# The reciprocal square roots of ten norms moved from GpSimd to ScalarE and VectorE, and two products to other PSUM banks, in a four-layer encoder trunk on one core

## The chip, the cores and the metric

The kernel runs on one core of one Trainium2 chip. The metric is the device time of one execution in microseconds (us). Three runs of the kernel before took 1830.92, 1827.35 and 1828.51 us, a median of 1828.51 us. The engines are named as the profile names them: PE (TensorE products), PEld (TensorE weight loads), DVE (VectorE), ACT (ScalarE), POOL (GpSimd), SP (SyncE, which issues the transfers).

## The reference

512 tokens of width 1024 pass through two layers. Each layer is half a SwiGLU, a mixer, and another half SwiGLU, and every one of these begins with an RMS norm over the width:

```python
def rms_norm(x, g):
    return x * rsqrt(mean(x * x, axis=-1) + 1e-6) * g
def swiglu(x, w_gate, w_up, w_down):          # 1024 -> 2816 -> 1024
    return (silu(x @ w_gate) * (x @ w_up)) @ w_down
for layer in range(2):
    h = h + 0.5 * swiglu(rms_norm(h), ...)
    h = h + mixer[layer](rms_norm(h), ...)    # 0: pooling and forgetting attention
    h = h + 0.5 * swiglu(rms_norm(h), ...)    # 1: latent attention, with two norms inside
out = rms_norm(h)
```

The mixer of layer 0 joins pooled means with 8 heads of attention whose logits carry sums of log forget gates (one Sigmoid per frame and head). That of layer 1 is attention with 16 heads over a compressed query (256 wide) and compressed keys and values (128 wide); each of the two has an RMS norm of its own. All is float32.

## The kernel before

Activations lie with the width on the 128 partitions (8 chunks, `h`) and the 512 tokens along the columns. Float32 products are made from two parts of each operand, a rounded one and the rest: `hi` is an ACT copy (L158), `lo` a DVE subtraction (L163, L165), and `mm3` issues three PE products for a block (L176 to L178). Weights come by SP in runs of 8 blocks (`raw`, three buffers), and are split by `split` or, in the feed-forward phases, by `unit`. In a part of the mixers' weights the subtraction is made on POOL instead (L205).

A norm's factor is not applied to the input of a projection but to its sums in PSUM, so that products can start before it is known. ACT squares each chunk of `h` as it becomes final, POOL (for the last chunk DVE) adds the squares up in `acc`, and `sums` turns them into the factor: products with a column of ones bring the sums to the tokens' partitions (L363), DVE divides and adds epsilon (L374), POOL raises to the power -0.5 (L375); `spread` then copies the factor to all partitions by products with the identity (L381) and an ACT copy to `rstdB` (L385). There are ten such norms: one ahead of each of the four feed-forward phases and two mixers, two inside the latent attention, and two at the end, where the output is normed in halves of the tokens. In the two at the end the last chunk's squares are not added to `acc` but summed by products of their own, and DVE adds the two sums (L370).

A feed-forward phase (`ffn`) makes gate and up products of two chunks of 128 hidden units at a time. The first pair of chunks is made by plain products: `begin` in the first phase, whose four sums lie in banks `pa`, `pa`, `px`, `pz`; `eight` in the other three, where all four sums take the two banks `pa` in turn, so that an up sum can start only when a gate sum has been read by DVE, times `rstdB` (L519). The other ten pairs are made by seven products of half size (`seven`, banks `px`, `py`, `pz`). Their right-hand factors (`right_factors`: L564 on ACT, L568 to L571 on DVE, and their splits) are made from `h` while the first pair's products run. Down products go to `pa` and are added to `h` by DVE (L602).

The order on each engine is made by the framework's list scheduler, which plays the program through a time model of its own, takes what is ready by priority (`soon` moves a step 400 places ahead), and then fixes the order of each engine's queue; at run time a queue waits at its head. `issue_after` adds an order behind a given instruction on that instruction's engine: the weights of the later pairs of heads in the latent attention (`keys_values`) have their POOL subtractions behind the last power. There `ordered` also fixes the order of products to the program's.

ACT holds one table of functions at a time. The profile shows seven ACT_TABLE_LOAD: one at the start (L222), three for Silu (L649), one each for Sigmoid (L870) and Exp in the two mixers (L784, L1250).

Of the kernel before, what the change touches and what calls it, by code (L numbers as in the profile page):

```python
# [34 lines left out]
# columns of the array of small parameters  # L35
# [22 lines left out]
# the order of the 1024 rows' chunks in a run of gate or up weights: pairs (2p, 2p + 1) of chunks  # L58
# are halves of the contraction
K_ORDER = (0, 2, 4, 6, 1, 3, 5, 7)  # L60
H = S // 2
# how much sooner than in the program's order the sums in PSUM are read
SOON = 400
# pairs of heads whose outputs are projected together, and how many chunks after a head's scores
MLA_GROUPS = ((0, 2), (2, 4), (4, 8))
EARLY = 1
# pairs of hidden chunks whose products are summed over together
GROUPS = ((0,), (1, 2), (3, 4), (5, 6), (7, 8), (9, 10))

# the causal layout of a head's 1280 score columns over three banks:  # L70
# query block -> (bank, first column)
SCORE_AT = ((1, 384), (2, 0), (1, 0), (0, 0))
# key block -> (bank, first column) of the transposed probabilities
PT_AT = ((0, 0), (1, 0), (2, 0), (1, 384))
PT_COLS = (512, 512, 256)
# forgetting attention: what the streamed column chunks are, and after which
# head's scores each of them is projected
# [9 lines left out]
def side_by_side(tile):  # L87
    """The two parts of the values of pairs of heads: [hi | lo] of one, [lo | hi] of the other."""
    v = tile.rearrange("p s n -> p (s n)")[:, 0:S].rearrange("p (q s c) -> p q s c", s=4, c=64)
    return v[:, :, ::3, :], v[:, :, 1:3, :]  # L90


# the banks of PSUM: rings of them in the feed-forward phases, and what the mixers take of them
# [4 lines left out]
class Trunk:  # L98
    def __init__(self, ctx, tc, d, out):
# [3 lines left out]
        self.pending = self.ordered = False  # L103
        self.state = ctx.enter_context(tc.tile_pool(name="state", bufs=1))
# [16 lines left out]
    @contextmanager  # L121
    def behind(self):
        """Work to be issued after that on the last chunk of the norm's input."""
        with ExitStack() as stack:
            for ins in self.last:
                stack.enter_context(self.tc.issue_after(ins.ins))
            yield
# [15 lines left out]
    def banks(self, **tags):  # L143
        """What a phase's kinds of sums take in turn of the banks."""
# [24 lines left out]
    def pe(self, ins):  # L169
        """Where the products' order is the program's."""  # L170
# [40 lines left out]
    def unit(self, src, blocks=8, piece=8, pool=False):  # L211
        """A run of 128x128 weight blocks from DRAM, split in two float32r parts."""
        return self.split(self.load(src, piece, blocks), piece, blocks, pool)

# [1 line left out]
    def setup(self):  # L216
        nc, d = self.nc, self.d
        k = self.keep
        # the table of activation functions comes in ahead of the data
        self.warm = k([P, 1], F32, "warm")  # L220
        nc.gpsimd.memset(self.warm, 0.0)
        nc.scalar.activation(self.warm, self.warm, AF.Copy)  # L222
# [3 lines left out]
        self.nhalf = k([P, TB], F32, "nhalf")  # L226
        nc.gpsimd.memset(self.nhalf, -0.5)
# [7 lines left out]
    def setup_tables(self):  # L235
        nc, d, k = self.nc, self.d, self.keep
        # tri[p, s] = 1 where p <= s
# [7 lines left out]
        # causal[p, s] = MASKED where s > p  # L245
# [9 lines left out]
        # sel8[p, h] = 1 where p is h, 32 + h, 64 + h or 96 + h  # L255
# [8 lines left out]
        # 1 over the counts of the pooling windows' first frames  # L264
# [9 lines left out]
    def rope_tables(self):  # L274
        """rope = [cos; +-sin; +-sin; cos], 32 rows each, frames along the columns: the steps."""
# [5 lines left out]
            # chunked[p, s] = MASKED where p < 64 <= s  # L281
# [31 lines left out]
        def angles():  # L313
            # cos(r) = sin(pi/2 - |r|)
# [15 lines left out]
    def square_into(self, src, first, last=False, part=slice(0, S)):  # L330
        """The last chunk's squares are kept apart: the sum over partitions takes both."""
# [14 lines left out]
    def prep(self, c, col):  # L346
        """Chunk c of h, times the norm's weight, in two parts."""
# [4 lines left out]
    def stats(self, n, rstdB):  # L352
        """From the squares: rsqrt(mean + eps), per token on partitions and as rows."""
        return self.sums(n)(rstdB)

    def sums(self, n):
        """The first part of it; what it returns does the second."""
# [3 lines left out]
        for i, sq in enumerate(self.squares):  # L361
            for t in range(blocks):
                self.pe(nc.tensor.matmul(ps[:, t * n_sq + i : t * n_sq + i + 1],  # L363
                                         sq[:, t * P : (t + 1) * P], self.ones[:, 0:1],
                                         start=True, stop=True))
        rt = self.ring("rt", 3, (P, TB))[:, 0:blocks]
        sums = ps[:, 0 : blocks * n_sq]
        if n_sq > 1:
            both = self.ring("both", 1, (P, TB))[:, 0:blocks]
            nc.vector.tensor_reduce(  # L370
                both, sums.rearrange("p (t i) -> p t i", i=n_sq), op=ALU.add, axis=AX.X
            )
            sums = both
        nc.vector.tensor_scalar(rt, sums, 1.0 / n, EPS, op0=ALU.mult, op1=ALU.add)  # L374
        self.power = nc.gpsimd.tensor_tensor(rt, rt, self.nhalf[:, 0:blocks], op=ALU.pow)  # L375

        def spread(rstdB):
            # every partition's copy of the tokens' values, by the identity
# [12 lines left out]
    def settle(self):  # L391
        """The norm that the last stage left to this one."""
        if self.pending:
            self.pending = False
            with self.soon():
                return self.stats(D, self.rstdB)

# [1 line left out]
    def ffn(self, f, col, next_col, start=False, rope=False):  # L399
        """Gate and up products of two chunks of 128 hidden units at a time, by Winograd's form of  # L400
        Strassen's seven products (but for the first two); the down products of a group of
# [1014 lines left out]
```

## Time and profile before

| what | us |
|---|---|
| median of three runs | 1828.51 (1827.35 to 1830.92) |
| the profiled execution: first to last instruction (its span) | 1824.4 |
| what lies between that span and the median | 4.1 |
| PE busy | 1753.3 |
| DVE busy | 1492.0 |
| ACT busy | 912.7 |
| POOL busy | 235.2 |

The profile comes from one execution; of that execution only the span is given, so the 4.1 us hold what lies around the span and the difference of one execution from the median. In a row of the timeline the first number is the start from the beginning of the span, the second the length; what stands in brackets is the idle time of that engine just before, and what ended it. `x3` is the number of instructions merged. The clock is that granted to TensorE, 1.00 being 2.4 GHz and 0.50 the lower level of 1.2 GHz; a window with 0.75 had each for half of its length.

### The profile page before, as it was taken

Reading aid. Unit: us, or ns where it says so; the run is one execution under the profiler, and the core shown is the slowest. Engines: PE = TensorE matmul, PEld = TensorE weight load, DVE = VectorE, ACT = ScalarE, POOL = GpSimd, SP = SyncE. Lnnn points to the kernel's source line nnn. Section 1 sums busy time; section 2 is a strip of 40 time slices with the busy share of each in tenths; the row PEclk is TensorE's granted clock in tenths of the full one; section 3 lists DMA queues with packets and bytes.
Section 4 is the critical chain, followed back from the end, with each engine's and each line's share of the span. In section 5 each row is a group of like instructions: output and inputs, shape, how many; then the busy total and the mean of one; then the engine's idle time right before and its main releaser. Section 6 shows DMA issues by size and latency. Waiting matters only on the chain.

```text
span 1824.4 us, 28424 instructions
## 1 busy us (share of the span) xinstructions
PE 1753.3 (96%) x11324; PEld 1585.1 (87%) x11324; DVE 1492.0 (82%) x2367; ACT 912.7 (50%) x1486; POOL 235.2 (13%) x165
## 2 busy tenths in 40 slices
PE   5999999999998999999999999999799989999998
PEld 4999999888787999999889999998677779999997
DVE  7998888648968988887779998964999789888873
ACT  6554444446645544444545444534677554444443
POOL 4000000113351000000200000003544310000002
PEclk8999999999999999999999999999999999999999
DMA  4233333313122333333223333241211123333331
GB/s 152 93 119 113 96 109 109 98 43 96 59 81 58 116 116 96 106 100 121 84 75 110 105 104 105 93 129 34 59 29 53 58 59 116 116 102 106 96 103 47
DMA packets 48933, 167.06 MB, mean 92 GB/s; under 512 B 5536, under 2 KB 7584, under 8 KB 48800
## 3 DMA queue, kind: packets, MB, share of 16 engines
q1 hardware_dynamic: 48800, 165.25, 30.0%
q8 instruction: 88, 1.44, 0.3%
q14 instruction: 45, 0.37, 0.1%
HBM read 163.14 MB, written 2.10 MB: 91 GB/s over the span
## 4 chain that ended last, share of the span: by engine, by line
PE 82%; DVE 10%; issue 3%; POOL 2%; ACT 2%; DMA 0%; SPq 0%; DVEq 0%; POOLq 0%; ACTq 0%
PE pa L176 11%; PE pa L177 11%; PE pa L178 11%; PE px L178 8%; PE px L176 8%; PE px L177 8%; PE pz L178 4%; PE pz L176 4%; PE pz L177 4%; PE py L178 2%; DVE pr L791 2%; PE py L176 2%; PE py L177 2%; POOL rt L375 2%; DVE mn L781 1%
## 5 line engine op out<-in xcount | busy, mean ns | idle before, releaser
L158 ACT ACTIVATE wh<-raw 128x1024 fp32r<-128x1024 f32 (+2 forms) x228 | 231.2, 1017 | 186.8 <-PE pa L177 77.0
L163 DVE TENSOR_TENSOR wl<-raw,wh 128x1024 fp32r<-128x1024 f32 (+1 forms) x195 | 234.5, 1205 | 24.7 <-ACT wh L158 24.1
L344 POOL TENSOR_TENSOR acc<-acc,sq 128x512 f32<-128x512 f32 (+1 forms) x48 | 63.0, 1313 | 1040.2 <-ACT sq L338 1039.7
L602 DVE SCALAR_TENSOR_TENSOR h<-pa,h 128x512 f32<-128x512 f32 (+1 forms) x200 | 132.8, 666 | 63.9 <-PE pa L178 62.7
L176 PE MATMUL pa<-hh,wh 128*128 128x512 f32 (+1 forms) x400 | 153.2, 383 | 0.0
L177 PE MATMUL pa<-hl,wh 128*128 128x512 f32 (+1 forms) x400 | 153.1, 383 | 0.0
L178 PE MATMUL pa<-hh,wl 128*128 128x512 f32 (+1 forms) x400 | 153.0, 383 | 0.0
L158 ACT ACTIVATE vh<-raw 128x1024 fp32r<-128x1024 f32 x88 | 93.2, 1059 | 88.9 <-PE px L177 37.4
L178 PE MATMUL px<-xh,wl 128*128 128x256 f32 (+1 forms) x456 | 129.9, 285 | 0.1
L177 PE MATMUL px<-xl,wh 128*128 128x256 f32 (+1 forms) x456 | 129.0, 284 | 0.0
L176 PE MATMUL px<-xh,wh 128*128 128x256 f32 (+1 forms) x456 | 128.8, 284 | 0.0
L177 PE MATMUL pa<-hl,vh 128*128 128x512 f32 (+1 forms) x336 | 128.0, 381 | 0.0
L176 PE MATMUL pa<-hh,vh 128*128 128x512 f32 (+1 forms) x336 | 127.7, 382 | 0.0
L158 ACT ACTIVATE wh<-s 128x1024 fp32r<-128x1024 f32 (+1 forms) x52 | 52.2, 1008 | 149.8 <-PE px L177 114.1
L178 PE MATMUL pa<-hh,vl 128*128 128x512 f32 (+1 forms) x336 | 125.7, 381 | 0.0
L163 DVE TENSOR_TENSOR vl<-raw,vh 128x1024 fp32r<-128x1024 f32 x88 | 107.2, 1219 | 11.8 <-ACT vh L158 11.7
L176 PE MATMUL pz<-eh,wh 128*128 128x256 f32 x384 | 107.6, 281 | 1.3 <-ACT wh L158 1.3
L177 PE MATMUL pz<-el,wh 128*128 128x256 f32 x384 | 107.4, 280 | 0.0
L178 PE MATMUL pz<-eh,wl 128*128 128x256 f32 x384 | 107.1, 279 | 0.0
L205 POOL TENSOR_TENSOR wl<-raw,wh 128x1024 fp32r<-128x1024 f32 (+2 forms) x33 | 75.4, 2292 | 130.4 <-ACT wh L158 127.1
L176 PE MATMUL px<-xh,sh 128*128 128x256 f32 x320 | 89.5, 280 | 0.0
L177 PE MATMUL px<-xl,sh 128*128 128x256 f32 x320 | 89.4, 279 | 0.0
(405 smaller groups left out, 5739.9 us busy)
## 6 DMA issues: line engine op xcount, KB each, us to landing
raw<-in_w_gu_dram SPq DMA_DIRECT2D x172, 512.0 KB, 3.6
raw<-in_w_dn_dram SPq DMA_DIRECT2D x88, 512.0 KB, 3.8
raw<-in_w_ab_dram SPq DMA_DIRECT2D x24, 512.0 KB, 3.6
raw<-in_w_mla_dram SPq DMA_DIRECT2D x12, 512.0 KB, 3.7
h<-in_x_dram SPq DMA_DIRECT2D x8, 256.0 KB, 5.7
raw<-in_w_qkv_dram SPq DMA_DIRECT2D x4, 448.0 KB, 3.3
raw<-in_w_gu_dram SPq DMA_DIRECT2D x6, 256.0 KB, 5.6
out_dram<-h SPq DMA_DIRECT2D x4, 384.0 KB, 3.0
```

Of the source, the lines that this page charges most:

```text
L158: return self.nc.scalar.activation(out, in_, AF.Copy, scale=scale)
L163: return nc.vector.tensor_tensor(out, in_, hi.bitcast(F32), op=ALU.subtract)
L176: self.pe(mm(out, ah, bh, start=start, stop=False, **kw))
L177: mm(out, ah, bl, start=False, stop=False, **kw)
L178: mm(out, al, bh, start=False, stop=stop, **kw)
L205: nc.gpsimd.tensor_tensor(l, r, h.bitcast(F32), op=ALU.subtract)
L344: (nc.vector if last else nc.gpsimd).tensor_tensor(acc, acc, sq, op=ALU.add)
L375: self.power = nc.gpsimd.tensor_tensor(rt, rt, self.nhalf[:, 0:blocks], op=ALU.pow)
L602: self.mark = nc.vector.scalar_tensor_tensor(h, ps, 0.5, h, op0=ALU.mult, op1=ALU.add)
L781: nc.vector.tensor_reduce(mn[:, i : i + 1], ps[:, cs], op=ALU.min, axis=AX.X)
L791: nc.vector.tensor_scalar(pr[bank][:, cs], pr[bank][:, cs], ri[:, i : i + 1], None, op0=ALU.mult)
```

## The change

The power goes. ACT reads the sums in PSUM three times: a square root (of four times the mean, that is twice the root), the mean plus epsilon, and the square of half the root. DVE adds the last two, takes a reciprocal and multiplies by the root: one Newton step on the table's square root. The two sums of squares at the end are summed in one PSUM column. The table of the square root is loaded ahead by a one-column ACT instruction (`table`) after the last hidden chunk of a phase or the last Exp of a mixer, and the next phase's table (Silu, Sigmoid or Exp, `then`) right behind the chain's last ACT step. The first pair's up sums in `eight` go to banks `px` and `pz`. The POOL subtractions of the latent attention are no longer ordered behind the power. (Comments and docstrings also go; line numbers move with them.)

```diff
-        nc.scalar.activation(self.warm, self.warm, AF.Copy)
+        nc.scalar.activation(self.warm, self.warm, AF.Sqrt)
...
+    def table(self, func, after):
+        with self.tc.issue_after(after.ins):
+            self.nc.scalar.activation(self.warm, self.warm, func)
...
-                self.pe(nc.tensor.matmul(ps[:, t * n_sq + i : t * n_sq + i + 1],
-                                         sq[:, t * P : (t + 1) * P], self.ones[:, 0:1],
-                                         start=True, stop=True))
-        rt = self.ring("rt", 3, (P, TB))[:, 0:blocks]
-        sums = ps[:, 0 : blocks * n_sq]
-        if n_sq > 1:
-            both = self.ring("both", 1, (P, TB))[:, 0:blocks]
-            nc.vector.tensor_reduce(
-                both, sums.rearrange("p (t i) -> p t i", i=n_sq), op=ALU.add, axis=AX.X
-            )
-            sums = both
-        nc.vector.tensor_scalar(rt, sums, 1.0 / n, EPS, op0=ALU.mult, op1=ALU.add)
-        self.power = nc.gpsimd.tensor_tensor(rt, rt, self.nhalf[:, 0:blocks], op=ALU.pow)
+                self.pe(nc.tensor.matmul(ps[:, t : t + 1], sq[:, t * P : (t + 1) * P],
+                                         self.ones[:, 0:1], start=i == 0 and t == 0,
+                                         stop=i == n_sq - 1, skip_group_check=True))
+        ms, root, rr, rt = (
+            self.ring(tag, 3, (P, TB))[:, 0:blocks] for tag in ("ms", "root", "rr", "rt")
+        )
+        act = nc.scalar.activation
+        act(root, ps[:, 0:blocks], AF.Sqrt, bias=self.eps[:, 1:2], scale=4.0 / n)
+        act(ms, ps[:, 0:blocks], AF.Identity, bias=self.eps[:, 0:1], scale=1.0 / n)
+        squared = act(rr, root, AF.Square, scale=0.5)
+        if then is not None:
+            self.table(then, squared)
+        nc.vector.tensor_tensor(rr, rr, ms, op=ALU.add)
+        nc.vector.reciprocal(rr, rr)
+        nc.vector.tensor_tensor(rt, root, rr, op=ALU.mult)
...
-            def eight(run, t):
+            def eight(run, t, tags):
                 for m in range(2):
-                    ps = self.project(*self.unit(run[m]), K_ORDER)
+                    ps = self.project(*self.unit(run[m]), K_ORDER, tag=tags[m])
...
-                            eight(run(n, i), t)
+                            eight(run(n, i), t, (("pa", "pa"), ("px", "pz"))[i])
...
+            self.table(AF.Sqrt, hidden)
...
-            t = scaled(latent(3, 5, lambda: spread_q.append(self.sums(2 * P))))
+            t = scaled(latent(3, 5, lambda: spread_q.append(self.sums(2 * P, AF.Exp))))
...
-                with ExitStack() as stack:
-                    if pair:
-                        stack.enter_context(self.tc.issue_after(self.power.ins))
+                if True:
...
+            self.table(AF.Sqrt, self.exp)
```

## Rows read from the trace of the kernel before

**Rows 1.** The page's first part: busy time, share, instructions of each engine
```profile
PE 1753.3 (96%) x11324; PEld 1585.1 (87%) x11324; DVE 1492.0 (82%) x2367; ACT 912.7 (50%) x1486; POOL 235.2 (13%) x165
```
**Rows 2.** What TensorE waited for: total us, times, longest
```profile
PE pc L381 <- POOL rt L375: 32.8, 5, 12.4
PE pa L176 <- DVE t L1216: 6.3, 1, 6.3
```
**Rows 3.** Timeline of PE, first spreading product of four norms: start, us, [idle before]
```profile
44.09 0.80 PE L381 MATMUL pc<-ident,rt 128*128 128x128 f32 x2 [12.39 <-POOL rt L375]
...
566.46 0.58 PE L381 MATMUL pc<-ident,rt 128*128 128x128 f32 x1 [6.85 <-POOL rt L375]
...
915.97 0.58 PE L381 MATMUL pc<-ident,rt 128*128 128x128 f32 x1 [5.13 <-POOL rt L375]
...
1477.61 0.58 PE L381 MATMUL pc<-ident,rt 128*128 128x128 f32 x1 [7.23 <-POOL rt L375]
```
**Rows 4.** Timeline of POOL at two powers, and of DVE beside the second
```profile
376.74 1.02 POOL L375 TENSOR_TENSOR rt<-rt,nhalf 128x4 f32<-128x4 f32 x1 [7.52 <-DVE rt L374]
...
560.05 6.35 POOL L375 TENSOR_TENSOR rt<-rt,nhalf 128x4 f32<-128x4 f32 x1 [11.34 <-DVE rt L374]
...
563.71 1.81 DVE L163 TENSOR_TENSOR el<-hl,eh 128x768 fp32r<-128x768 f32 x2
```
**Rows 5.** Windows behind those four waits: length, busy PE PEld DVE ACT POOL, clock
```profile
44.10:48.00 3.90, 3.90 (x20) 3.90 (x21) 1.16 (x2) 0.60 (x1) 0.00 (x0) 0.56 0.00 0
...
566.50:570.00 3.50, 3.50 (x17) 3.50 (x18) 0.80 (x2) 1.33 (x2) 0.00 (x0) 0.53 0.02 5
...
916.00:922.00 6.00, 6.00 (x30) 6.00 (x31) 2.15 (x3) 1.72 (x3) 0.00 (x0) 0.56 0.00 0
...
1477.60:1482.00 4.40, 4.39 (x24) 4.39 (x25) 1.65 (x3) 1.72 (x3) 0.00 (x0) 0.60 0.00 0
```
**Rows 6.** Timeline of PE, first and last of six neighbouring gate products
```profile
556.75 0.40 PE L176 MATMUL pa<-xh,wh 128*128 128x512 f32 x1
...
557.90 0.39 PE L178 MATMUL pa<-xh,wl 128*128 128x512 f32 x1
```
**Rows 7.** Windows at the four feed-forward starts, columns as in rows 5
```profile
31.70:90.00 58.30, 45.91 (x343) 44.38 (x343) 51.69 (x87) 29.05 (x42) 9.62 (x1) 0.88 0.29 91
546.00:590.00 44.00, 36.55 (x203) 32.20 (x204) 34.71 (x57) 26.18 (x38) 7.65 (x2) 0.92 0.23 66
590.00:620.00 30.00, 30.00 (x231) 28.83 (x230) 28.97 (x44) 16.43 (x24) 0.00 (x0) 1.00 0.32 92
896.00:940.00 44.00, 38.87 (x209) 34.27 (x209) 33.29 (x56) 23.66 (x36) 9.66 (x5) 0.92 0.23 66
1458.00:1500.00 42.00, 33.88 (x186) 29.55 (x186) 33.37 (x55) 24.99 (x37) 7.64 (x2) 0.92 0.21 64
```
**Rows 8.** Groups by line, ACT then DVE: count, busy us, mean ns, idle before
```profile
L649 ACT ACT_TABLE_LOAD x3 | 3.8, 1283 | 0.1
...
L868 ACT ACTIVATE f<-f 128x32 f32<-128x32 f32 x1 | 0.2, 219 | 0.0
...
L874 DVE TENSOR_TENSOR f<-f,f 128x32 f32<-128x32 f32 x1 | 0.2, 191 | 0.0
```
**Rows 9.** Timeline of POOL, then of DVE, at the latent attention's rotary key
```profile
1274.71 5.63 POOL L205 TENSOR_TENSOR wl<-raw,wh 128x640 fp32r<-128x640 f32 x3
...
1275.68 0.69 DVE L1110 TENSOR_TENSOR t<-pa,rstdB 128x512 f32<-128x512 f32 x1 [2.02 <-PE pa L178]
1276.40 2.50 DVE L1139 TENSOR_TENSOR t<-t,rope 128x512 f32<-128x512 f32 x1
...
1282.21 1.48 DVE L1149 TENSOR_SCALAR rota<-rkv 64x512 f32<-64x512 f32 x1
...
1284.32 0.42 DVE L1149 TENSOR_SCALAR rotb<-rkv 64x512 f32<-64x512 f32 x1
```
**Rows 10.** Timeline of PE, the last norm's spreading products
```profile
1816.11 1.22 PE L381 MATMUL pc<-ident,rt 128*128 128x128 f32 x4 [1.24 <-POOL rt L375]
```

More of the change, by code (lines that the diff above doesn't have):

```diff
@@ L103, in __init__ @@
         self.pending = self.ordered = False
+        self.then = None
         self.state = ctx.enter_context(tc.tile_pool(name="state", bufs=1))
@@ L225, in setup @@
         make_identity(nc, self.ident)
-        self.nhalf = k([P, TB], F32, "nhalf")
-        nc.gpsimd.memset(self.nhalf, -0.5)
+        self.eps = k([P, 2], F32, "eps")
+        nc.gpsimd.memset(self.eps[:, 0:1], EPS)
+        nc.gpsimd.memset(self.eps[:, 1:2], 4.0 * EPS)
         self.ones = k([P, P], F32, "ones")
@@ L350, in prep, with stats, sums @@
         return self.lo(self.xl[c], self.h[c], self.xh[c], scale=g)
-    def stats(self, n, rstdB):
-        return self.sums(n)(rstdB)
-    def sums(self, n):
+    def stats(self, n, rstdB, then=None):
+        return self.sums(n, then)(rstdB)
+    def table(self, func, after):
+        with self.tc.issue_after(after.ins):
+            self.nc.scalar.activation(self.warm, self.warm, func)
+    def sums(self, n, then=None):
         nc = self.nc
@@ L395, in settle @@
             with self.soon():
-                return self.stats(D, self.rstdB)
+                return self.stats(D, self.rstdB, self.then)
     def ffn(self, f, col, next_col, start=False, rope=False):
@@ L407, in tile_ @@
                 return pool.tile(list(shape), dt, name=self.name(tag), tag=tag, bufs=bufs)
-            self.pool, self.temps = pool, 0
+            self.pool, self.temps, self.then = pool, 0, AF.Silu
             if start:
@@ L654, in ffn @@
                     hh, hl = tile_("hh", 4, (P, 2, S), F32R), tile_("hl", 4, (P, 2, S), F32R)
-                    self.hi(hh, u)
+                    hidden = self.hi(hh, u)
                     self.lo(hl, u, hh)
@@ L706, in next, with project @@
             self.square_into(self.h[c], c == 0, c == KC - 1)
-    def project(self, wh, wl, order=tuple(range(KC)), at=None, then=None):
-        ps = self.bank("pa")
+    def project(self, wh, wl, order=tuple(range(KC)), at=None, then=None, tag="pa"):
+        ps = self.bank(tag)
         for b, k in enumerate(order):
@@ L783, in probabilities @@
             bank, ps, cs = sc[i]
-            nc.scalar.activation(
+            self.exp = nc.scalar.activation(
                 pr[bank][:, cs], ps[:, cs], AF.Exp, bias=mn[:, i : i + 1],
@@ L911, in pool_fox @@
             self.banks(**MIXER_BANKS)
-            self.pool, self.temps = pool, 3
+            self.pool, self.temps, self.then = pool, 3, AF.Sigmoid
             def ptile(tag, bufs=1, dt=F32R, shape=(P, S)):
@@ L1135, in mla @@
             cq.append(parts(1, scaled(ps, False), C_QN + 1))
-            sqi = self.last[-1]
             spread_q = []
-            t = scaled(latent(3, 5, lambda: spread_q.append(self.sums(2 * P))))
+            t = scaled(latent(3, 5, lambda: spread_q.append(self.sums(2 * P, AF.Exp))))
             nc.vector.tensor_tensor(t, t, self.rope, op=ALU.mult)
@@ L1247, in head_values @@
                     self.lo(yl[pair], self.y, yh[pair])
-            with self.tc.issue_after(sqi.ins):
-                nc.scalar.activation(self.warm, self.warm, AF.Exp)
             keys_values(0)
@@ L1274, in mla @@
                 done = (head, self.transposed(pool, pr))
+            self.table(AF.Sqrt, self.exp)
             for chunk in early:
```

## The prediction, made before any run of the change

> **What bounds the kernel now.** I read the page's busy times first. PE is busy for 1753.3 of 1824.4 us and DVE for 1492.0 [rows 1], so the kernel is a stream of products with about 71 us of holes, and a change that shortens no product can only fill holes. The list of what PE waited for says where they are: 32.8 us in five waits, all for the power, the longest 12.4; the next entry has 6.3 us, in the latent attention [rows 2]. No other cause is near these two.
>
> The timeline then puts each wait in its place. The four long ones are the starts of the four feed-forward phases: 12.39, 6.85, 5.13 and 7.23 us, together 31.6 [rows 3]. PE's queue stands at the first spreading product and holds everything behind it. The fifth, 1.24 us, is at the end [rows 10].
>
> Why does a power over four columns take 6.35 us there, and 1.02 us ahead of the first mixer [rows 4]? The reader should look at DVE beside it. At 560.05 the power starts; DVE runs its splits without a pause until 563.71 + 1.81 = 565.52 us; the power ends at 566.40, 0.88 us later, about the length of an undisturbed one [rows 4]. The same pattern stands at all four starts. So POOL is shut out while DVE works on two operands in SBUF, and the factor comes when DVE runs out of work, not when it is wanted. In the other direction the same is seen in the latent attention: three POOL subtractions from 1274.71 to 1280.34, and beside them a DVE product of 128x512 that takes 2.50 us where the one ahead of it takes 0.69 [rows 9].
>
> Last I read the clock. Behind each of the four waits the granted clock is 0.56, 0.53, 0.56 and 0.60 for 3.9, 3.5, 6.0 and 4.4 us although PE is busy [rows 5]: it had fallen to 1.2 GHz during the wait and came back to 2.4 GHz late. A wait thus costs its length plus the share of that window that was lost.
>
> **The change part by part.** *The four feed-forward starts.* The prices before are, wait plus window times one minus its clock: first phase 12.39 + 3.9 x 0.44 = 14.1 us; second 6.85 + 3.5 x 0.47 = 8.5; third 5.13 + 6.0 x 0.44 = 7.8; fourth 7.23 + 4.4 x 0.40 = 9.0 [rows 3, 5].
>
> The new chain has three ACT steps and three DVE steps. The nearest rows are 0.219 us for an ACT step and 0.191 us for a DVE one, both of 128x32 [rows 8], so its length is 3 x 0.22 + 3 x 0.19 = 1.2 us if nothing stands ahead of it in the two queues; with one long split of about 1 us ahead of it on each, some 3 us. None of it is on POOL, so DVE can no longer shut it out.
>
> What covers it? In the last three phases the up sums now have banks of their own and PE can go on without the factor. Six neighbouring products of this size start from 556.75 to 557.90, 0.23 us apart [rows 6]; two up sums have 48 of them, so 11 us of cover, more than 3. The PE wait should vanish there, and with it the fall of the clock. What is late next is DVE: it used the wait to make right-hand factors and weight splits, and has the same work to do in less time. That sets what can be kept. In the second phase's start DVE is busy for 34.71 of 44 us, in the third's 33.29 of 44, in the fourth's 33.37 of 42 [rows 7]. While it works off what is left, in the 30 us behind, it reaches 28.97 of 30, 97% [rows 7]. With three steps added (0.57 us) and 97% as the most it can do, the same work needs 36.5, 35.1 and 35.1 us. That would keep 7.5 of 8.5, all of 7.8 (it could give 8.9) and 6.9 of 9.0: 22.2 us. Bounds: 25.3 if DVE's lateness never reaches PE, about half if it does throughout.
>
> In the first phase there is no such cover from banks: its up sums were already apart and done before the wait. Here PE needs the splits that DVE makes during the wait. From 31.7 to 90 us DVE is busy for 51.69 of 58.30 [rows 7], so only 6.6 us are to be had, less 0.57: 6.0 at full use, 4.2 at 97%. I take 5 of the 14.1; bounds 3 and 14.1, the upper one if PE can use what DVE has made so far.
>
> *The latent attention.* Three POOL subtractions were queued behind the last power and ran from 1274.71 for 5.63 us, beside four DVE operations from 1276.40 to 1283.69 [rows 9]. Undisturbed, at 0.69 and 0.42 us for the two sizes, the four would take about 2.2 us, so 5.1 us were lost, and PE waits 6.3 us for the result [rows 2]. Without the order behind the power I expect two of the three to go earlier and one (1.9 us) to stay: a gain of 3.2. Against that, early subtractions can now stand beside the Newton steps of the inner norms, whose add and multiply have two operands in SBUF as the disturbed product has, and each meeting costs up to 2.50 - 0.69 = 1.8 us in a stretch whose product order is fixed. I take one of these at half price off, and put the gain at 2; bounds minus 3.4 (three meetings of 1.8, with 2 gained) and plus 6.3.
>
> *The end.* The wait of 1.24 us [rows 10] held a reduction, a DVE step and the power; three ACT and three DVE steps make 1.23. Nothing; bounds minus and plus 0.5 for each of the two halves. The first half's chain has the second half's products beside it, as before.
>
> *The mixers' own first norms.* No wait for the power stands in the list for them beyond the five, so nothing is gained; the chain is no longer than the power's, so nothing is lost.
>
> *Table loads.* Before there are seven. After, by the code, fourteen: the square root ahead of every group of norms and the phase's own function behind it. Each is 1.283 us [rows 8]. I cost the seven new ones at nothing. The square root's load stands behind the last hidden split of a phase, where ACT (912.7 us busy in all) has only squares and copies to make; that of Silu stands where ACT has no reader. Without that cover each would cost 1.28 us, 9.0 together.
>
> The Trainium skill (ScalarE: Activation LUTs, section "What ACT_TABLE_LOAD costs") speaks against this change: a switch of table is put there at 1283 ns plus 1380 ns for the engine to drain. By it, the seven new switches would come to 18.6 us as an estimate, if every one of them held up PE. The trace agrees on the load and shows no such drain ahead of one: 0.1 us idle before three loads together [rows 8].
>
> **The sum.** 22.2 + 5 + 2 + 0 = 29.2 us. Against the profiled span that is 1824.4 - 29.2 = 1795.2; the median of the runs lies 4.1 us above that span, so 1828.5 - 29.2 = 1799.3 us.
>
> **The rivals.**
>
> *DVE takes the place of the power.* Behind the second phase's start DVE is at 97% for 30 us while PE never waits [rows 7]; with PE some 8 us ahead, weight splits come just too late and the holes return in small pieces. For: DVE's 82% overall [rows 1], and the exact fit above. Against: PE held no wait for splits in that stretch. Half of the 27.2 us would go: 1828.5 - 13.6 - 2 = 1813. Chance 17%.
>
> *All of it is hidden,* the first phase too, since lower priority splits can wait: 25.3 + 14.1 + 2 = 41.4, so 1787. For: PE has banks free there once the first four sums are read. Against: DVE's record there. Chance 12%.
>
> *The loads hold up the queue* and PE waits for each of the seven: 1799.3 + 9.0 = 1808. Against: the loads stand where ACT has idle time. Chance 5%.
>
> *No change.* The scheduler fixes the queue by its own times; if it puts the spreading product as early as now and ACT's or DVE's part of the chain late, PE stands as long as before. It would give 1828. Against: it would take a delay of 5 us and more in queues whose single instructions are about 1 us. Chance 5%.
>
> *Slower: the table thrashes.* Copy, Square and the table functions share a table in every phase seen, since seven loads serve them all; Sqrt and Identity are not in this trace. If Sqrt's table lacked one of the others, loads would alternate at 1.283 us. It makes the kernel slower by the bound below once it costs 29.2 + 3.7 us, that is from 26 loads on that nothing covers, about three for each norm; with four for each, 40 x 1.283 = 51 us, it gives 1851. Chance 4%.
>
> **How the numbers follow.** The forecast has the rest, 57%, with a range of its own of 1792 to 1806 (22.2 between 17 and 25.3, the other terms by 3 to 4 us either way). I predict 1799. To hold 8 in 10, the range reaches over the cases of a late DVE and of all hidden: 1785 to 1815. The time of this kernel can be told from no change at about 0.2%, 3.7 us. Faster by more: 57 + 17 + 12 + 5 = 91%; same 5%; slower 4%.
>
> **What would show it.** Right: no POOL instruction left in the chain; PE's waits for the spreading product under 1 us at 566, 916 and 1477 (each earlier by what went before), with the clock at 1.00 through these starts; in the first phase a rest of some 5 to 9 us, now for a DVE split; DVE at 97% and above in the windows of rows 7; DVE's product at L1139 at 0.69 us or with one wait of about 1.8; fourteen table loads. Wrong: more than fourteen loads; waits of PE for `wl`, `el` or `sl` in the 60 us behind each start, adding up to more than 5 us a phase; or new waits inside the two mixers, where the scheduler has made another order.

## The result, and the profile after

The changed kernel takes 1804.04 us (median of four) against 1827.93 us for the kernel before beside it: a ratio of 0.9861, 95% interval [0.9844, 0.9877]. One of the four runs, and one of the kernel with ACT copies below, was disturbed (3482.40 and 4688.88 us); the ratios leave these two out, and without them the medians are 1802.87 us (1801.93 to 1805.21) and 1799.18 us. 1799 was forecast for the change, with a range of 1785 to 1815. The profiled execution has a span of 1801.2 us against 1824.4. The page's busy line and the head of the list of what TensorE waited for (total us, times, longest) answer to [rows 1, 2]:

```profile
PE 1750.9 (97%) x11324; PEld 1581.2 (88%) x11324; DVE 1496.9 (83%) x2385; ACT 927.8 (52%) x1534; POOL 198.9 (11%) x156
```
```profile
PE pa L177 <- ACT wh L159: 6.3, 2, 5.9
PE pa L177 <- DVE t L1225: 4.6, 1, 4.6
...
PE px L179 <- DVE wl L164: 3.5, 2, 3.2
PE pz L177 <- ACT g L505: 3.1, 2, 1.6
PE px L177 <- ACT wh L159: 3.0, 1, 3.0
...
PE px L177 <- ACT g L498: 1.8, 2, 1.6
...
PE pc L391 <- DVE rt L385: 1.3, 1, 1.3
```

The first of these is the kernel's own start and was there before. PE was busy for 1753.3 us and is for 1750.9, so its holes went from 71.1 to 50.3 us: 20.8 of the 23.2 us are holes. Of the 32.8 us of waits for the factor 1.3 us are left in this list, and 0.8 in one of the latent attention's norms (below). The first spreading products (timeline; start, us) show no wait at any of the four starts, and one at the end:

```profile
45.49 0.72 PE L391 MATMUL pc<-ident,rt 128*128 128x128 f32 x5
...
567.11 1.05 PE L391 MATMUL pc<-ident,rt 128*128 128x128 f32 x8
...
914.45 1.05 PE L391 MATMUL pc<-ident,rt 128*128 128x128 f32 x8
...
1465.98 1.05 PE L391 MATMUL pc<-ident,rt 128*128 128x128 f32 x8
...
1793.46 0.68 PE L391 MATMUL pc<-ident,rt 128*128 128x128 f32 x4 [1.28 <-DVE rt L385]
```

The windows behind the last three of those starts, as in [rows 5], and then windows as long as those of [rows 7]. These begin 0.4 to 2.1 us ahead of the last add of squares; those of [rows 7] began 4.9 us behind it at the first start and some 5 us ahead of it at the other three:

```profile
567.10:570.60 3.50, 3.50 (x33) 3.50 (x32) 3.46 (x7) 2.72 (x4) 0.00 (x0) 1.00 0.04 9
914.40:920.40 6.00, 5.75 (x49) 5.54 (x49) 5.67 (x9) 3.55 (x7) 0.00 (x0) 1.00 0.42 165
1466.00:1470.40 4.40, 4.40 (x39) 4.34 (x38) 4.37 (x7) 3.28 (x5) 0.00 (x0) 1.00 0.24 42
```
```profile
26.60:84.90 58.30, 49.28 (x351) 45.53 (x351) 56.68 (x100) 31.75 (x50) 0.00 (x0) 0.94 0.27 82
547.40:591.40 44.00, 42.45 (x275) 38.46 (x274) 43.23 (x73) 29.13 (x47) 0.00 (x0) 1.00 0.30 96
591.40:621.40 30.00, 30.00 (x223) 28.47 (x222) 27.67 (x43) 14.95 (x21) 0.00 (x0) 1.00 0.28 89
891.00:935.00 44.00, 43.75 (x274) 39.25 (x273) 43.57 (x74) 30.40 (x49) 0.00 (x0) 1.00 0.25 78
1447.00:1489.00 42.00, 40.45 (x260) 36.56 (x259) 41.25 (x72) 28.50 (x46) 0.00 (x0) 1.00 0.30 95
```

The clock is 1.00 behind the three, where it was 0.53 to 0.60, and DVE, the third busy column, is full: 43.23 of 44, 43.57 of 44, 41.25 of 42. In the windows of [rows 7] moved by exactly as much as the last adds (543.9, 887.8 and 1443.7 us on) it is 42.44, 41.83 and 41.04 us, 95 to 98%. By stage, cut where DVE adds the last squares into `acc` (times of those rows: 26.82 to 1462.74 before, 27.03 to 1448.48 after; PE idle is the window's length less PE's busy time in it; FFN is a feed-forward phase):

| stage | before, us | after | difference | predicted | PE idle before | after |
|---|---|---|---|---|---|---|
| up to the first add | 26.82 | 27.03 | +0.21 | 0 | 6.22 | 6.65 |
| first FFN | 342.48 | 340.28 | -2.20 | -5 | 12.39 | 9.02 |
| first mixer | 182.29 | 182.19 | -0.10 | 0 | 2.91 | 2.32 |
| second and third FFN | 699.48 | 683.64 | -15.84 | -15.3 | 12.45 | 1.80 |
| latent attention | 211.67 | 215.34 | +3.67 | -2 | 20.21 | 20.08 |
| fourth FFN and end | 361.66 | 352.72 | -8.94 | -6.9 | 16.97 | 10.43 |
| span | 1824.4 | 1801.2 | -23.2 | -29.2 | 71.15 | 50.30 |

### The profile page after: what moved, and what is told of

Read it like the earlier page. It is cut to its first block, busy times and chain, and to the rows that moved or that the text cites. A ratio compares the mean times of both kernels' runs of the same rounds, so it can differ in the third digit from the quotient of the medians.

```text
span 1801.2 us, 28499 instructions
## 1 busy us (share of the span) xinstructions
PE 1750.9 (97%) x11324; PEld 1581.2 (88%) x11324; DVE 1496.9 (83%) x2385; ACT 927.8 (52%) x1534; POOL 198.9 (11%) x156
## 4 chain that ended last, share of the span: by engine, by line
PE 81%; DVE 14%; ACT 2%; issue 2%; DMA 1%; SPq 0%; POOL 0%; DVEq 0%; ACTq 0%; POOLq 0%
PE pa L177 11%; PE pa L178 11%; PE pa L179 11%; PE px L177 8%; PE px L179 8%; PE px L178 8%; PE pz L177 4%; PE pz L179 4%; PE pz L178 4%; DVE pr L802 2%; PE py L177 2%; PE py L179 2%; PE py L178 2%; DVE mn L792 1%; DVE wl L164 1%
## 5 line engine op out<-in xcount | busy, mean ns | idle before, releaser
L179 PE MATMUL px<-xh,wl 128*128 128x256 f32 (+1 forms) x480 | 138.4, 289 | 3.5 <-DVE wl L164 3.5
L177 PE MATMUL px<-xh,wh 128*128 128x256 f32 (+1 forms) x480 | 137.2, 288 | 3.0 <-ACT wh L159 3.0
L178 PE MATMUL px<-xl,wh 128*128 128x256 f32 (+1 forms) x480 | 137.8, 288 | 0.0
L177 PEld LDWEIGHTS px<-xh,wh 128*128 128x128 f32 x480 | 90.1, 189 | 7.3 <-ACT wh L159 3.4
L179 PEld LDWEIGHTS px<-xh,wl 128*128 128x128 f32 x480 | 90.7, 189 | 6.4 <-DVE wl L164 4.1
L178 PEld LDWEIGHTS px<-xl,wh 128*128 128x128 f32 x480 | 90.5, 188 | 2.8
```

The lines of the kernel that those rows point to most:

```text
L177: self.pe(mm(out, ah, bh, start=start, stop=False, **kw))
L178: mm(out, ah, bl, start=False, stop=False, **kw)
L179: mm(out, al, bh, start=False, stop=stop, **kw)
```

## The experiments

Each time stands against the kernel before in the runs beside it (1827.57 to 1828.58 us); stages are cut as in the table. In the expectations MLA is the latent attention.

**One half of the change at a time.** First the changed kernel with its first pair's up sums back in `pa`:

```
-    eight(run(n, i), t, (("pa", "pa"), ("px", "pz"))[i])
+    eight(run(n, i), t, (("pa", "pa"), ("pa", "pa"))[i])
```


> The changed kernel with the up sums of the first pair back in the two banks pa. If the cover by banks is what lets PE go on while the chain runs (in the changed kernel the chain takes about 9 us from its first ACT step to its last DVE step at the second phase's start, because DVE splits stand between its steps), PE stands there again for 5 us or more at each of the three later starts, with a fall of the clock, and the time is about 1820 to 1826 us. Rival: the shorter way around POOL is what gains, and the banks add little: 1804 to 1808 us. The first phase and the latent attention should keep their stage times either way.

Measured: 1819.61 us, ratio 0.9953 [0.9941, 0.9966]. Then the kernel before with the banks alone, the power still on POOL:

```
-    eight(run(n, i), t)
+    eight(run(n, i), t, (("pa", "pa"), ("px", "pz"))[i])
...
-        ps = self.bank("pa")
+        ps = self.bank(tag)
```


> The kernel before with nothing changed but the banks of the up sums (px, pz); the power stays on POOL. If POOL is shut out for as long as DVE has work, the power ends only when DVE pauses, and with 11 us more of products ahead of PE's spreading products the wait at each later start falls from 5 to 7 us to 0 to 3: about 1808 to 1816 us, the first start still with its 12.4 us wait. Rival: the power is pushed back by as much as the cover grows, since DVE has work for all of it, and the waits stay: 1825 us and above.

Measured: 1822.22 us, 0.9962 [0.9947, 0.9977], between the two expectations. The chain alone gives some 9 us, the banks alone some 6, both together 24 to 26: neither half has most of the gain. With the chain alone PE stands for splits in pieces; its idle time is 4.3, 3.3 and 5.0 us in the three later FFN stages, a little under the 5 us expected, and the clock falls at the second and the fourth FFN's start and not at the third FFN's. With the banks alone PE still waits 11.6, 5.5, 2.3 and 5.6 us for the power at the four starts. Why the power is still late is in this kernel's timelines of POOL, DVE and PE at the second start:

```profile
561.23 9.28 POOL L375 TENSOR_TENSOR rt<-rt,nhalf 128x4 f32<-128x4 f32 x1 [11.34 <-DVE rt L374]
```
```profile
568.08 1.22 DVE L163 TENSOR_TENSOR wl<-raw,wh 128x1024 fp32r<-128x1024 f32 x1
569.22 0.42 DVE L163 TENSOR_TENSOR xl<-hl,xh 128x256 fp32r<-128x256 f32 x1
```
```profile
570.56 0.80 PE L381 MATMUL pc<-ident,rt 128*128 128x128 f32 x2 [5.53 <-POOL rt L375]
```

The cover that the banks give PE gives DVE more to do as well, and the power, 6.35 us long in [rows 4], now takes 9.28. It ends at 570.51, 0.87 us behind the last split of DVE's train (569.22 + 0.42 = 569.64); in [rows 4] it was 0.88 us. The Trainium skill (SBUF — State Buffer, section "Who interferes with whom") lets a VectorE operation with two SBUF inputs contend with a GpSimd one that reads SBUF, and calls this contention an exclusive lock. The trace agrees, but here one power stays out over the whole train of operations, not over one.

**The latent attention.** It came out 3.67 us longer, so three kernels changed only that part. One brings back the power for its three norms (and its tile of exponents) and the order of the later weights behind the last of them:

```
-            spread = self.sums(D)
+            spread = self.sums(D, power=True)
...
-                if True:
+                with ExitStack() as stack:
+                    if pair:
+                        stack.enter_context(self.tc.issue_after(self.power.ins))
```


> The changed kernel, but the three norms of the latent attention use the power on POOL again, with the later pairs' POOL subtractions queued behind the last of them, as before. The stage from the norm ahead of the latent attention to the one behind it took 211.67 us before and 215.34 after the change. If the loss of 3.7 us comes from the chain and order in the beginning of this stage, the stage falls back to about 211.7 and the kernel to about 1800.4 us. Rival: it comes from elsewhere (the square root's table load at the end of the stage, or a queue order further on that is fixed by chance): stage 214 to 216, time 1804 us.

Measured: 1796.51 us, 0.9822 [0.9809, 0.9836], some 6 to 7 us better than the change and 4 us better than expected; the latent attention's stage is 212.77. Of the 6.5 us between the two profiles only 2.6 lie in this stage. The rest lies outside it, and the end of the next section says where. The second keeps the Newton chain and holds those weights behind the query norm's Square:

```
-        squared = act(rr, root, AF.Square, scale=0.5)
+        self.power = squared = act(rr, root, AF.Square, scale=0.5)
```


> The changed kernel with one thing undone in the latent attention: the weights of the later pairs of heads are again ordered behind the last inner norm, here behind its last ACT step, so that their ACT copies and with them the POOL subtractions come after it. If the early subtractions are what costs (the changed kernel shows DVE's add of squares at 2.03 us in place of 0.69, and two waits of PE for the chain, 0.80 and 0.23 us), the stage falls from 215.3 to about 212 to 213 us and the kernel to about 1801. Rival: later subtractions only move the meeting with DVE to the rotary key, as before the change, and the stage stays at 215 or grows: 1804 to 1806 us.

Measured: 1807.44 us, 0.9884 [0.9869, 0.9898]; the stage is 218.28, longer as the rival had it, and more so. A third is the power in these norms without the order; its edit stands against the first of these kernels:

```
-                with ExitStack() as stack:
-                    if pair:
-                        stack.enter_context(self.tc.issue_after(self.power.ins))
+                if True:
```


> The e3 kernel (MLA's three norms by the GpSimd power, the FFN's by root and Newton step), but without the order that holds the later pairs' weight splits behind MLA's last power. Tells apart which of the two of e3 gave back MLA's 2.6 us (215.3 to 212.8). Theory: the order did it, because without it the splits of the second pair's weights stand in front of the heads' work on ScalarE and VectorE; then MLA's stage is 215 or more here and the time 1799 to 1803 us. Rival: the power did it, because it takes the three Newton chains off ScalarE and VectorE; then the stage stays at 212 to 213 and the time at 1796 to 1798 us.

Measured: 1800.55 us, 0.9846 [0.9831, 0.9861]; the stage is 220.2 in the profile. That is the theory's stage and time, and looks like the order's doing, but PE's idle time there is 20.5 us (220.0 less 199.48 busy, 1230 to 1450 us) against 19.6 in the kernel with the order, so almost all of the 7.4 us between the two profiles is busy time. 5.1 us of it are the clock: in this stage it is at its lower level for 20.5 us against 10.2, and half of the difference is lost. The rest may be the order's: all four runs of this kernel lie above all four of the other (1794.91 to 1797.36). This kernel's runs go from 1798.28 us at a mean granted clock of 0.992 to 1803.89 at 0.989, the profiled one. So we looked at the clock and ran both kernels again.

**Both kernels once more.** No edit.

> The changed kernel as it is, executed again. Theory: MLA's stage (215.34 us in the first profile, 211.67 before the change) is 208 to 210 us of work plus half of the time for which TensorE's granted clock is at half (13.7 us of it in the first profile, 6.8 before), and how often the clock falls there differs by execution: the stage moves by 1.7 us for each 3.4 us at half clock, and stage less half of that time stays at 208 to 210. Rival: the order of the queues sets it; then the stage repeats at 215 to 216 us with the same waits, whatever the clock.

> The kernel before as it is, executed again. Theory (the clock's draw): MLA's stage less half of its time at half clock is 208 to 210 us again (208.25 in the first profile), and the stage itself may come out up to 5 us longer than 211.67. The half-clock stretches behind the three waits for the power at the later FFN starts come again, 6.8 us each or one step of 3.4 less. Rival: all of it repeats within 0.5 us, stage and stretches.

Measured: the change 1802.71 us, 0.9863 [0.9849, 0.9878], its stage 215.32; the kernel before 1828.64 us, 1.0003 [0.9994, 1.0013], but its stage now 214.50 in place of 211.67. PE's waits in it are the same: the stage's idle time is 20.21 and 20.06 us. The difference is in the clock column. Two windows of the latent attention's heads, from the first profile of the kernel before, the second one, and, for the first window, the change:

```profile
1300.00:1325.00 25.00, 21.53 (x126) 17.87 (x126) 24.47 (x58) 19.19 (x51) 15.50 (x11) 1.00 0.13 37
1385.00:1410.00 25.00, 20.89 (x120) 16.77 (x121) 23.15 (x50) 17.63 (x45) 11.44 (x7) 1.00 0.21 62
```
```profile
1300.00:1325.00 25.00, 21.53 (x117) 17.72 (x117) 23.25 (x53) 17.72 (x46) 13.90 (x11) 0.93 0.13 40
1385.00:1410.00 25.00, 22.45 (x122) 17.66 (x121) 21.93 (x47) 16.82 (x41) 13.00 (x8) 0.93 0.14 42
```
```profile
1300.00:1325.00 25.00, 21.69 (x115) 17.96 (x116) 22.30 (x47) 19.08 (x48) 13.18 (x10) 0.93 0.09 27
```

A window of 25 us at 0.93 has lost 1.75 us, two of them 3.5. So 2.8 of the 3.67 us belong to the first profile of the kernel before, whose clock did not fall at these places; 0.8 us are left between the second profiles. The clock theory has the kernel before right in kind: less half of its 13.7 us at the lower clock the stage is 207.7 us, 0.3 under the range given. For the change it forbade nothing that happened: its four runs lie within 0.22 us, and the stage came again with the same falls, as the rival had it. Over all thirteen profiles the stage goes from 211.7 to 220.2 us, and less half of its time at the lower clock from 207.7 to 211.0.

**The first start.** The low parts of the right-hand factors go from DVE to an ACT copy there (the subtraction is left out):

```
-    self.lo(self.el[p], t[:, 0:3, :], self.eh[p])
+    if start:
+        self.hi(self.el[p], t[:, 0:3, :])
```


> The changed kernel, but in the first FFN the low parts of the right-hand factors are made by a ScalarE copy in place of the VectorE subtraction (the subtraction is left out there, so these low parts hold another value); nothing else differs. Theory: what the change did not gain at the first start (2.0 of 5 us) is held back by VectorE, which is full from 26 to 48 us with splits, among which the three steps of the factor wait. With the subtractions gone TensorE's wait for a low part of the weights (3.16 at 40.22) and the lateness of the factor at 45.49 shrink: 3 to 6 us off the first stage, 1798 to 1801 us in all. Rival: ScalarE's high parts bound this start (TensorE's wait of 3.00 at 34.92 is for one of them), and copies put on ScalarE make them later: the first stage is the same or up to 4 us longer, 1804 to 1808 us.

Measured: 1800.00 us, 0.9838 [0.9823, 0.9853]. The first FFN's stage is 336.68, 3.6 us shorter, and PE's idle time in it 5.09 in place of 9.02; the 3.16 us wait for a `wl` is gone, the one for a `wh` is 3.28. The spreading product starts at 42.01 in place of 45.49. The theory holds: the copies put on ACT lengthened the wait for `wh` by only 0.3 us.

**The chain's length.** The Newton step is left out, in all norms:

```
-        act(root, ps[:, 0:blocks], AF.Sqrt, bias=self.eps[:, 1:2], scale=4.0 / n)
-        act(ms, ps[:, 0:blocks], AF.Identity, bias=self.eps[:, 0:1], scale=1.0 / n)
-        squared = act(rr, root, AF.Square, scale=0.5)
+        squared = act(root, ps[:, 0:blocks], AF.Sqrt, bias=self.eps[:, 0:1], scale=1.0 / n)
...
-        nc.vector.tensor_tensor(rr, rr, ms, op=ALU.add)
-        nc.vector.reciprocal(rr, rr)
-        nc.vector.tensor_tensor(rt, root, rr, op=ALU.mult)
+        nc.vector.reciprocal(rt, root)
```


> The changed kernel with the Newton step left out: ScalarE's root and VectorE's reciprocal are the whole chain (the mean, the square, the sum and the product are gone), in all norms. Theory: the chain of six steps takes 9 to 16 us at the FFN starts because its VectorE steps wait their turn among splits, and only where TensorE comes to the factor's products before it is ready does that cost: about 2 us at the first start, 0.8 in MLA's second norm and 1.2 at the end, nothing at the other three starts, where TensorE stood for nothing: 1800 to 1802 us. Rival: the steps themselves cost VectorE and ScalarE time at every start, whether or not TensorE waits for them, so that each of the four starts gives 1 to 2 us more: 1794 to 1799 us.

Measured: 1793.75 us, 0.9808 [0.9795, 0.9822], below both expectations, nearer to the rival. The first stage loses 3.8 us, the second FFN's 1.8, the third's 0.35, the fourth's with the end 2.6. (The profile is that of the slowest of its five runs, 1798.13 us; its latent attention takes 219.1 us, with 20.5 us at the lower clock.) Factor and product at the first two starts (timelines of PE):

```profile
38.49 2.04 PE L386 MATMUL pc<-ident,rt 128*128 128x128 f32 x8 [0.38 <-DVE rt L380]
...
559.31 0.94 PE L386 MATMUL pc<-ident,rt 128*128 128x128 f32 x7
```

With the last adds at 27.12 and 545.82 the spreading product comes 11.4 and 13.5 us after them; in the change it is 18.5 and 17.6. PE did not wait for the factor there in the change either. What it waited for, 1.55 us at 574.45, was ACT's reading of a bank (the `g` of L505 in the list above), and that wait is gone too: PE's idle time in the second and third FFN is 0 in place of 1.80. So what the Newton step cost there came through the readers of the banks. That the late factor alone put them back is not shown: just ahead of that read ACT stood 1.91 us for a transfer of weights, and with two steps ACT's queue has another order there:

```profile
573.06 1.06 ACT L159 ACTIVATE wh<-raw 128x1024 fp32r<-128x1024 f32 x1 [1.91 <-DMA raw<-in_w_gu_dram]
574.03 0.37 ACT L505 ACTIVATE g<-pz 128x256 f32<-128x256 f32 x1
```

**Table loads where they fall.** The change without its own loads ahead:

```
-        with self.tc.issue_after(after.ins):
-            self.nc.scalar.activation(self.warm, self.warm, func)
+        pass
```


> The changed kernel without its own table loads ahead: each load comes where the first function that needs another table stands, so a square root's load lies in the chain, between the squares' sums and the root, and a Silu's or an exponential's load before its first use. Theory: the loads ahead hide 1.28 us each where TensorE waits for the chain: the end (1.3 us), MLA's norms (up to 1.3) and perhaps 0 to 2 us over the first start; at the other starts nothing, since the factor is in time there with several us to spare: 1804 to 1808 us. Rival (the loads ahead hold the ScalarE queue, as one of the forecast's rivals had it): without them the splits behind each load run 1.3 us sooner, and the time is 1798 to 1802 us.

Measured: 1807.46 us, 0.9892 [0.9877, 0.9908]: 4.75 us slower than the change. There are fourteen loads again, but one now stands among ACT's readers of the banks at the first start (timeline of ACT):

```profile
50.92 1.28 ACT L658 ACT_TABLE_LOAD   x1
52.22 0.63 ACT L658 ACTIVATE g<-g 128x512 f32<-128x512 f32 x1
```

PE's wait for a reader there grows from 0.65 to 2.01 us, and behind it the granted clock is 0.51 for 3.5 us (timeline of PE):

```profile
53.17 0.48 PE L177 MATMUL px<-xh,vh 128*128 128x256 f32 x1 [2.01 <-ACT g L507]
```

Of the 5.2 us between the two profiles the first FFN has 2.8, the latent attention 0.8 and the fourth FFN with the end 0.9. The loads ahead are worth their place.

**The best of both.** The power in the latent attention with its order, root and reciprocal without a Newton step elsewhere:

> Root and reciprocal alone at the FFN starts, the mixer of the second stage and the end (Newton step left out), and MLA's three norms by the GpSimd power as in the kernel before, with the order of MLA's later weights behind the last power. Theory: the gains add, since they lie in different stages: the e3 kernel's 1796.5 less what leaving out the Newton step gives outside MLA (1 to 3 us by the first theory of it), 1793 to 1796 us, MLA's stage at 212 to 213. Rival: the stage of MLA moves by several us with any change of the queues' order, and what e3 showed was such a draw: 1797 to 1803 us, MLA's stage at 214 or more.

Measured: 1791.25 us, 0.9794 [0.9780, 0.9807], the fastest, below both expectations; its latent attention takes 215.9 with three falls of the clock, as the rival had it. So the shorter stage of the kernel with the power did not come again. Of the kernels that keep the Newton step, that one is the fastest, but most of what it gains lies outside the latent attention.

## Why the prediction came out

The total was right for its first reason: the waits for the power went away and the clock no longer falls behind the three later starts. The sum against the profiled span was 1795.2, 6.0 us too low, and three terms make that up.

- **The three later starts: 22.2 forecast, 24.8 measured** (15.84 + 8.94, with the end in it). DVE is at 95 to 99% there, by where the window is put, as forecast (97%), but its lateness hardly reached PE: 1.80 us of idle time in two stages. That is near the bound of 25.3, not the middle. The rival of DVE in the power's place fell here.
- **The chain: 1.2 to 3 us forecast, 9.4 us measured.** This step failed, though the time hung little on it. At the second start ACT's steps follow each other at once (timelines of ACT and of DVE), DVE's do not:

```profile
555.65 0.24 ACT L377 ACTIVATE root<-pc,eps 128x4 f32<-128x4 f32 x1
555.80 0.25 ACT L378 ACTIVATE ms<-pc,eps 128x4 f32<-128x4 f32 x1
555.95 0.20 ACT L379 ACTIVATE rr<-root 128x4 f32<-128x4 f32 x1
556.16 1.28 ACT L361 ACT_TABLE_LOAD   x1
557.46 0.20 ACT L361 ACTIVATE warm<-warm 128x1 f32<-128x1 f32 x1
```
```profile
560.09 0.15 DVE L383 TENSOR_TENSOR rr<-rr,ms 128x4 f32<-128x4 f32 x1
...
562.50 0.16 DVE L384 RECIPROCAL rr<-rr 128x4 f32<-128x4 f32 x1
...
564.90 0.15 DVE L385 TENSOR_TENSOR rt<-root,rr 128x4 f32<-128x4 f32 x1
```

  Each DVE step has a place of its own in the queue, with some 2.3 us of splits ahead of it. The factor is ready at 565.05, 15.6 us behind the last add (549.50); by the power it was 566.40 - 551.59 = 14.8. So the factor does not come sooner. What the change brings is that it comes at a fixed place in DVE's queue while DVE and PE both work, and that PE has products until then. That is why each half alone gave about a third or less: banks alone put the power off by 3 us more, the chain alone leaves PE at the splits.
- **The first start: 5 forecast, 2.2 measured.** The reason given, DVE's splits, was right for one of the two long waits, and is shown by the ACT copies; the other wait is for a split on ACT. DVE reached 97% (56.68 of 58.30) over the whole window, but PE stood for 3.00 + 3.16 us early in it (timeline of PE). The clock still fell behind the first of these waits (0.51 from 37.0 to 43.9 us, with PE busy for 3.7 us of it), so nothing of the 1.7 us that it cost before came back. PE's idle time in the stage fell by 3.4 us and its busy time rose by 1.2, for which no run here shows a reason. The factor came at 44.78: three `wh` splits separate ACT's steps (root at 32.79, square at 36.66), and DVE's add comes behind its own splits at 42.37. PE did not wait for it:

```profile
34.92 0.39 PE L177 MATMUL px<-xh,wh 128*128 128x256 f32 x1 [3.00 <-ACT wh L159]
...
40.22 0.58 PE L179 MATMUL px<-xh,wl 128*128 128x256 f32 x1 [3.16 <-DVE wl L164]
```

- **The latent attention: -2 forecast, +3.67 in the first profiles, +0.8 in the second.** One meeting of the rotary product with a POOL subtraction of weights stayed, as costed. What the term had wrong is the rest of that train. It laid all 5.1 us lost before to the three subtractions of weights, but from 1280.29 on two other POOL subtractions, which are not of weights (`xl`, L1191), stood beside DVE. The change keeps them (L1200), and beside them two DVE operations lose some 2 us again, 1.49 us in place of 0.42 and 1.66 in place of 0.69 (timelines of POOL before, then of POOL and DVE after):

```profile
1280.29 3.12 POOL L1191 TENSOR_TENSOR xl<-t,xh 64x512 fp32r<-64x512 f32 x2
```
```profile
1259.64 1.55 POOL L206 TENSOR_TENSOR wl<-raw,wh 128x640 fp32r<-128x640 f32 x1 [4.52 <-ACT wh L159]
1262.58 2.88 POOL L1200 TENSOR_TENSOR xl<-t,xh 64x512 fp32r<-64x512 f32 x2 [1.39 <-ACT xh L159]
```
```profile
1259.78 1.96 DVE L1150 TENSOR_TENSOR t<-t,rope 128x512 f32<-128x512 f32 x1
...
1262.83 1.49 DVE L1160 TENSOR_SCALAR rota<-rkv 64x512 f32<-64x512 f32 x1
1264.34 1.66 DVE L1163 SCALAR_TENSOR_TENSOR rota<-rkv,rope 64x512 f32<-64x512 f32 x1
```

  The wait for the rotary product fell from 6.3 to 4.6 us [rows 2], less than the 3.2 us costed, and 0.80 us came in at the second norm (L391 at 1247.57). The early subtractions met no Newton step, but one met the add of squares at 1253.63 (2.03 us in place of 0.69), for which PE waited 0.23. The heads' stretch, which I had left out, took the rest: PE's idle time over the stage is 20.21 before and 20.08 after. What is left of the first comparison, some 3 us, is busy time at the lower clock, which the sum had no term for.
- **Table loads: nothing forecast, none seen.** Twelve loads stand at L361, one each at L223 and L795, 1.283 us each, and no wait of PE is put down to one. The Trainium skill (ScalarE: Activation LUTs, section "What ACT_TABLE_LOAD costs") adds 1380 ns of drain to each; the load of 556.16 starts 0.01 us behind the Square and the next function starts at 557.46, so the trace agrees with its load and shows no drain.
- **The end: nothing forecast,** and the wait is 1.28 us where it was 1.24 [rows 10].

One thing stays open in part. The kernel with the power in the latent attention is also 1.0 to 1.6 us faster in the first, second and fourth FFN, whose queues have the same order, and this came again in its variant without the order (341.80 and 341.84 us for the second FFN, against 343.38 and 343.58 in the change's two profiles). The gain is in the products: the same unbroken run of 157 products of 256 columns, at a clock of 1.00, takes 18.37 us from its first start to its last in the change and 18.21 in that kernel, 117.8 against 116.7 ns each (timelines of PE in the two):

```profile
825.63 0.28 PE L177 MATMUL pz<-eh,wh 128*128 128x256 f32 x1
...
844.00 0.28 PE L178 MATMUL px<-xl,sh 128*128 128x256 f32 x1
```
```profile
823.36 0.28 PE L177 MATMUL pz<-eh,wh 128*128 128x256 f32 x1
...
841.57 0.28 PE L178 MATMUL px<-xl,sh 128*128 128x256 f32 x1
```

An FFN stage has 1680 such products or more, which makes some 1.9 us as an estimate. The three kernels with the power in the latent attention have the shorter interval there; the kernel before and all the others have the longer one. What sets it no run here tells.

## What to carry to other kernels

A short chain among long work is as long as the queues that it shares: count what stands ahead of each step, and ask what the waiting engine can do until then, before asking how fast the steps are. Two edits that each move the bound to the other's place may give little alone and much together, so test them together as well. And before a stage's difference of a few microseconds is explained by the order of its queues, look at the clock column and profile the unchanged kernel twice.

## What the runs showed of the hardware

- The granted clock fell in one execution and not in another of the same kernel, behind the same waits: in the window from 1300 to 1325 us TensorE waited 1.66 and 1.65 us for the same `pr` in the two profiles of the kernel before, and the window ran at 1.00 and at 0.93.
- A power over 128x4 took 1.02 us undisturbed, 6.35 and 9.28 us beside VectorE operations with two operands in SBUF, and ended 0.88 and 0.87 us behind the last of the train each time.
- The same 157 products of 256 columns in the same order, at a granted clock of 1.00, came every 117.8 ns in one kernel and every 116.7 ns in another.
